# Soft-routing mixture of experts on one core: five instead of four pairs of P1 in front, four instead of six mixed stages, six instead of five pairs of P2, and B21's casts spread over 56 slots instead of 44

## The chip, the core and the metric

The kernel runs on one core of a Trainium2 chip. The metric is the device time of one execution in microseconds (us). The core's engines are named as in its profile: PE (TensorE, the matrix unit; PEld is its weight load), DVE (VectorE), ACT (ScalarE), POOL (GpSimd, which here only issues DMAs, those with a change of type among them) and SP (SyncE, which issues DMAs). Each engine takes its instructions strictly in order. SBUF is the on-chip memory that all engines read, PSUM the accumulator memory that PE writes (eight banks of 128 x 512 float32 here).

## The reference

```
batch, seq, hidden, n_experts, expert_hidden = 16, 512, 512, 8, 2048
probs = softmax(router_logits)                  # over the 8 experts
for e in range(n_experts):
    expert_out = np.matmul(x, expert_weights[e])
    output += probs[:, :, e:e+1] * expert_out
```

All 8 experts see every token. Scaling a token's row of x by its probability and putting the eight scaled copies side by side makes it one product: a left matrix of 8192 rows (tokens) by 4096 (8 experts x 512 hidden) with the stacked weights, 4096 by 2048. Inputs and output are float32; the products run in float16 with float32 sums.

## The kernel before

**Two levels of Strassen's method (Winograd's form).** At the upper level the rows are split into 16 blocks q of 512 tokens, each with an even and an odd half of 256 tokens; the contraction is split into the experts 0 to 3 and 4 to 7; the output columns into two halves of 1024. A weight quadrant is B11, B12, B21 or B22 (first digit the half of the experts, second digit the half of the columns). Seven products P1 to P7 for each q take the place of eight. P1 is x's even half, scaled by the probabilities of the experts 0 to 3, times B11; P2 is the same rows, scaled for the experts 4 to 7, times B21. The first output block of a q is P1 + P2. P1 alone is needed again later, in the base of P6, and so goes to a DRAM buffer `kept` as well.

**One product** (`Product`) is again seven inner steps, in the order of `STEPS` (1, 5, 6, 2, 7, 3, 4). A step is eight 128x128 by 128x512 matmuls into one PSUM bank. Its left operand is a tile `z` (or `d`, a difference) that DVE makes from x and the probabilities (`Left`, `times`), its right operand a weight tile `w`. Each product gives four output tiles `h` of 128 x 512 float32, called (0, 0), (0, 1), (1, 0), (1, 1). A product without a base (P1) leaves PSUM by ACT copies and two DVE additions (`post_alone`). A product with a base (P2) takes the base tile, already in SBUF, and DVE adds PSUM to it in place at six of the seven steps (`post_on_base`). A finished tile is stored by `pool(...)`, a DMA on POOL's queue.

**Stages.** `add(product, product)` makes a stage of two products, whose steps take turns: 14 slots of one step. In the trace a stage of two products takes 24.17 us, a slot 1.73 us. P1 of q = 0 and 1 is computed in a plain way in the beginning, before stage 0. Stages 0 to 3 are pairs of P1 (q = 2 to 9), stages 4 to 9 are mixed (P2 of q beside P1 of q + 1, for q = 9 to 14), stages 10 to 14 are pairs of P2 alone (15 and 0, 1 and 2, and so on to 7 and 8). After them come the pairs of P5 and P6, of P6 and P7, P4 and P7, and P3.

In a mixed stage the base of P2 of q is the tile `h` in which P1 of the same q was left one stage before, `products[1, q].o`, which stays in SBUF. In a pair of P2 the base has to be read back from `kept` by a DMA on SP's queue (`Base.fetch`, `fetch_at`), except for q = 15. x blocks work alike: a mixed stage reuses the transposed block `xT` of P1, a pair of P2 alone loads it again from DRAM (`x_dram`).

**Hooks and weights.** `at(stage, slot, make)` hangs work at a slot. The four blocks of B21 are cast from float32 to float16 by DMAs on POOL's queue (`cast21`, two DMAs of 512 KB each), `sums_at` puts the three sums of them (2.28 us of DVE each, in place of four tiles seven) in the last stage of P1 pairs. From the first mixed stage on, six "wedges" (`wedge_at`) follow at one for each stage: at slot 2 two casts of 512 KB, at slot 11 three DVE operations (1.21 us each) whose results go to DRAM in three stores of 512 KB (`wd`); B12 and B22 give the later right operands t1, t2, t3 this way. The part ODD of these is cast apart: B12 at stage 9 slot 9, B11 at stage 10 slot 2, B22 at stage 10 slot 9 (`cast_odd`, two DMAs of 512 KB each), combined by three DVE operations of 2.28 us from stage 11 slot 6 on (`odd_t`). Stage 11 also fetches three t1 blocks of 1 MB on ACT's queue (`fetch_at_w`).

**Buffers and queues that set the order.** `hpool` has 12 buffers for `h`; `wpool` has 15 for `w`. A fetch of a base takes the next buffer of `hpool`, and SP waits until the store that read the buffer last has landed. POOL's DMAs use eight semaphores in turn, so that each waits until the one eight before it has landed: at most eight are under way. DVE's work is put in order by a small planner (`later`, `slack`, `need`) that knows a cost for each task and a clock for PE.

Of the kernel before, what the change touches and what calls it, by code (L numbers as in the profile page):

```python
# [31 lines left out]
def kernel(  # L32
# [87 lines left out]
    def pool(o, i, **how):  # L120
        note(nc.gpsimd.dma_start(out=o, in_=i, **how))  # L121
# [26 lines left out]
    def cast_block(q, kn, t=None, parts=1):  # L148
        t = new_w() if t is None else t
        for e in range(2):  # L150
            cast_w(q, kn, e, t[:, ds(e * C, C), :], parts if e == 0 else 1)
        return t
# [204 lines left out]
    def need(task):  # L357
        if task is not None and not task.done:
            flush(task)
            clock["pe"] = max(clock["pe"], clock["dve"])  # L360

    def later(cost, make, first=False):
        t = Task(cost, make)
        (queue.appendleft if first else queue.append)(t)
        return t
# [181 lines left out]
                tt(o[tn], q if p in (5, 3) else x, base, ADD)  # L547


    def out_rows(q, odd, cols, tn):  # L550
        t, n = tn
        return out_f[ds((2 * q + odd) * HQ + t * HP, HP), ds(cols * NH + n * NB, NB)]

    def to_out(q, odd, cols, **how):
        return lambda tn, o: pool(out_rows(q, odd, cols, tn), o, **how)
# [20 lines left out]
    def at(stage, slot, make):  # L576
        hooks.setdefault((stage, slot), []).append(make)

    def add(*products):
        stages.append(products)  # L580
        return len(stages) - 1
# [11 lines left out]
    def left_of(r, q, fresh=True):  # L593
        a, b = 2 * q, 2 * q + 1
        if r == 1:
            pt = PBlock(a, P1, xp1[q - 2][1] if q in (2, 3) else None)
            if q in (2, 3):
                xs[a] = XBlock(a, xp1[q - 2][0])
            return Left(xblock(a), pt), [xblock(a), pt]
        if r in (2, 4):  # L600
            h, pt = (a, PBlock(a, P2)) if r == 2 else (b, PBlock(b, P2))
            return Left(xblock(h), pt), [xblock(h), pt]
        if r == 5:
            pt = PBlock(b, PQ)
            return Left(xblock(b), pt), [xblock(b), pt]
        if r == 6:
            pt = PBlock(a, P1)
            return Left(xblock(a), pt, of=lefts[5, q]), [xblock(a), pt]
        pa, pb = PBlock(a, P1 if r == 7 else PQ), PBlock(b, P1 if r == 7 else PQ)
        return Left(xblock(a), pa, (xblock(b), pb)), [xblock(a), pa, xblock(b), pb]  # L610

    def kept_rows(q):
        return lambda tn: kept[q][tn[1], ds(tn[0] * HP, HP), :]

    def product(r, q, **how):
        left, loads = left_of(r, q)
        lefts[r, q] = left
        p = None
        if r == 1:
            def sink(tn, o):  # L620
                pool(kept_rows(q)(tn), o)
            p = Product(right[1], left, sink)
        elif r == 2:
            if q >= 9:
                base = products[1, q].o.__getitem__
            else:
                base = bases[2, q] = Base(kept_rows(q))
            p = Product(right[2], left, to_out(q, 0, 0), base)
        elif r == 5:
            bases[6, q] = m1 = Base(kept_rows(q))  # L630
            m1.task = {}

            p = Product(right[5], left, to_out(q, 1, 0))
        elif r == 6:
            m1 = bases[6, q]

            def base(tn):
                need(m1.task[tn])
                return m1.t[tn]
            p = Product(right[6], left, to_out(q, 0, 1), base)  # L640
        elif r == 7:
            base = bases[7, q] = Base(lambda tn: out_rows(q, 0, 1, tn))
            p = Product(right[7], left, to_out(q, 1, 1), base)
        elif r == 4:
            p = Product(right[4], left, to_out(q, 1, 0, accum_op=ADD), products[7, q].o.__getitem__)
        else:
            p = Product(right[3], left, to_out(q, 0, 1, accum_op=ADD), **how)
        p.loads = loads
        products[r, q] = p
        return p  # L650

    products = {}
    forget = lambda *hs: [xs.pop(h, None) for h in hs]
# [53 lines left out]
    def fetch_at(stage, slot, base, *tns):  # L707
        for tn in tns:
            at(stage, slot, lambda tn=tn: base.fetch(tn))


    for q in (2, 4, 6, 8):
        add(product(1, q), product(1, q + 1))
    for q in range(9, 15):
        add(product(2, q), product(1, q + 1))
    forget(*range(0, 18, 2))
    rest = [15] + list(range(9))
    for i in range(0, 10, 2):
        k = add(product(2, rest[i]), product(2, rest[i + 1]))
        for slot, tn in zip((8, 10, 12, 13), INNER):  # L720
            for q in rest[i:i + 2]:
                if q < 9:
                    fetch_at(k if tn == (1, 0) else k - 1, 3 if tn == (1, 0) else slot, bases[2, q], tn)
    xs.clear()
    k5 = add(product(5, 0), product(5, 1))
# [37 lines left out]
    def wedge(kn, e):  # L763

        t = new_w()
        a, b = t[:, ds(0, C), :], t[:, ds(C, C), :]
        rows = ds(e * C, C)

        def casts():
            cast_w(12, kn, e, a)  # L770
            cast_w(22, kn, e, b)

        def send(what, u):
            pool(kept_w(what, kn)[:, rows, :], u)

        def t3():
            u = new_u().rearrange("p (c two) t -> p c (two t)", two=2)
            tt(u, b, a, SUB)
            send("t3", u)

        def t1():
            tt(a, b11[kn][:, rows, :], a, SUB)
            send("t1", a)

        def t2():
            tt(b, b, a, ADD)
            send("t2", b)
        return casts, [t3, t1, t2]

    def wedge_at(stage, slot, kn, e, then):  # L790
        made = []

        def begin():
            casts, made_ = wedge(kn, e)
            casts()
            made.extend(made_)

        def go_on():
            for make in made:
                later(1.22, make)  # L800
        at(stage, slot, begin)
        at(*then, go_on)

    b21, t1, t2, t3 = {}, {}, {}, {}

    def cast21(kn):
        b21[kn] = cast_block(21, kn)

    for i, kn in enumerate(((0, 0), (0, 1), (1, 1), (1, 0))):
        at((11 * i + 8) // 14, (11 * i + 8) % 14, lambda kn=kn: cast21(kn))  # L810

    def sums_at(stage, slot, r, of, ps):
        def go():
            if right[r].w is None:
                right[r].sums = right[r].build(of)
            for p in ps:
                right[r].queue_sum(right[r].sums, p)
        at(stage, slot, go)
    sums_at(3, 3, 2, b21, (5,))
    sums_at(3, 5, 2, b21, (6,))  # L820
    sums_at(3, 7, 2, b21, (7,))
    sums_at(3, 12, 2, b21, (4,))
    for i, (kn, e) in enumerate((kn, e) for kn in ((0, 0), (1, 0), (1, 1)) for e in range(2)):
        wedge_at(4 + i, 2, kn, e, (4 + i, 11))

    def fetch_at_w(stage, slot, of, what, kn):
        at(stage, slot, lambda: of.__setitem__(kn, fetch_w(what, kn)))
# [141 lines left out]

    finish = products[3, 15]  # L970
    finish.base = Base(lambda tn: out_rows(15, 0, 1, tn))
    finish.sink = lambda tn, o: sp(out_rows(15, 0, 1, tn), o)
    for slot, tn in zip((6, 8, 10, 12), INNER):
# [73 lines left out]
```

## Time and profile before

| what | value |
|---|---|
| median of 3 runs | 1375.59 us (1375.47 to 1375.77) |
| the profiled execution | 1376.63 us, its span (first to last instruction) 1374.9 us |
| mean granted TensorE clock | 1.000 |
| PE busy | 1367.3 us, 99% of the span |
| DVE busy | 1108.6 us, 81% |
| POOL busy (issuing DMAs) | 411.8 us, 30% |
| ACT busy | 183.1 us, 13% |
| moved by DMA | 338.02 MB, mean 246 GB/s |

Busy times are sums over one engine; an engine can be busy while nobody waits for it. A wait is told as "who waited <- what ended the wait". The stages below are told by their place in the span: stage 0 begins at 41.0 us, and each stage of two products is 24.17 us long, so that stage 9 is 258.60 to 282.77, stage 10 is 282.77 to 306.94, stage 11 is 306.94 to 331.12 and stage 12 is 331.12 to 355.29. A DMA has a time of issue and a time of landing; the time between the two is told with it.

### The profile page before, as it was taken

Reading aid. Unit: us, or ns where it says so; the run is one execution under the profiler, and the core shown is the slowest. Engines: PE = TensorE matmul, PEld = TensorE weight load, DVE = VectorE, ACT = ScalarE, POOL = GpSimd, SP = SyncE. Lnnn points to the kernel's source line nnn. Section 1 sums busy time; section 2 is a strip of 40 time slices with the busy share of each in tenths; the row PEclk is TensorE's granted clock in tenths of the full one; section 3 lists DMA queues with packets and bytes.
Section 4 is the critical chain, followed back from the end, with each engine's and each line's share of the span. In section 5 each row is a group of like instructions: output and inputs, shape, how many; then the busy total and the mean of one; then the engine's idle time right before and its main releaser. Section 6 shows DMA issues by size and latency. Waiting matters only on the chain.

```text
span 1374.9 us, 17480 instructions
## 1 busy us (share of the span) xinstructions
PE 1367.3 (99%) x6390; PEld 622.0 (45%) x6390; DVE 1108.6 (81%) x1290; ACT 183.1 (13%) x317; POOL 411.8 (30%) x652
## 2 busy tenths in 40 slices
PE   8999999999999999999999999999999999999998
PEld 4444444444444444444444444444444444444444
DVE  5846757669889888798897988889889898988882
ACT  3222111100011111111111100000000000222221
POOL 3222333241223342334232122242333322232221
PEclk9999999999999999999999999999999999999999
DMA  9998999999898998899898998988898979987786
GB/s 183 222 261 205 211 248 265 241 299 378 240 323 249 285 300 246 259 261 265 245 276 263 338 392 219 224 236 212 229 237 223 247 204 316 249 187 177 166 150 106
DMA packets 191271, 338.02 MB, mean 246 GB/s; under 512 B 52944, under 2 KB 86992, under 8 KB 187472
## 3 DMA queue, kind: packets, MB, share of 16 engines
q0 software_dynamic: 88688, 185.12, 55.8%
q1 hardware_dynamic: 98464, 123.34, 30.8%
q10 hardware_dynamic: 4032, 28.44, 5.3%
q8 instruction: 50, 0.82, 0.2%
q14 instruction: 37, 0.30, 0.1%
HBM read 207.65 MB, written 156.43 MB: 265 GB/s over the span
## 4 chain that ended last, share of the span: by engine, by line
PE 98%; DMA 2%; POOL 0%; issue 0%; ACT 0%; POOLq 0%
PE ps L127 98%; DMA w<-wd 1%; DMA w<-in_expert_weights_dram 1%; POOL w L121 0%; ACT h L999 0%; POOL ident L211 0%; POOLq L211 0%; POOLq L1031 0%
## 5 line engine op out<-in xcount | busy, mean ns | idle before, releaser
L127 PE MATMUL ps<-w,z 128*128 128x512 f16 x5416 | 1177.3, 379 | 1.3 <-DMA w<-in_expert_weights_dram 1.1
L127 PEld LDWEIGHTS <-z 128*128 128x128 f16 x5416 | 529.7, 98 | 638.6 <-DMA w<-in_expert_weights_dram 1.3
L121 POOL DMA_DIRECT2D out_dram<-h x380 | 248.9, 672 | 746.4 <-ACT h L540 373.7
L107 DVE TENSOR_TENSOR h<-ps,h 128x512 f32<-128x512 f32 x415 | 282.5, 687 | 207.6 <-PE ps L127 192.8
L107 DVE TENSOR_TENSOR z<-xT,pT 128x2048 f16<-128x2048 f16 x220 | 266.8, 1216 | 11.5 <-DMA xT<-xs 6.3
L127 PE MATMUL ps<-w,d 128*128 128x512 f16 x880 | 199.1, 379 | 0.0
L127 PEld LDWEIGHTS <-d 128*128 128x128 f16 x880 | 86.1, 98 | 103.8
L107 DVE TENSOR_TENSOR z<-z,d 128x2048 f16<-128x2048 f16 x110 | 132.1, 1215 | 0.0
L107 DVE TENSOR_TENSOR w<-w 128x1024 f16<-128x1024 f16 (+2 forms) x92 | 100.8, 1102 | 5.1 <-DMA wd<-w 3.4
L527 ACT COPY h<-ps 128x512 f32<-128x512 f32 x90 | 52.8, 586 | 373.4 <-PE ps L127 336.3
L540 ACT COPY h<-ps 128x512 f32<-128x512 f32 x64 | 37.5, 587 | 486.3 <-PE ps L127 459.9
L107 DVE TENSOR_TENSOR d<-z 128x1024 f16<-128x1024 f16 x110 | 75.2, 685 | 6.8 <-PE ps L127 5.0
L107 DVE TENSOR_TENSOR z<-z,u 128x2048 f16<-128x2048 f16 x64 | 78.4, 1225 | 2.2
L107 DVE TENSOR_TENSOR u<-xT,pT 128x2048 f16<-128x2048 f16 x64 | 77.9, 1217 | 0.0
L523 ACT COPY h<-ps 128x512 f32<-128x512 f32 x90 | 52.8, 587 | 173.9 <-PE ps L127 162.5
L121 POOL DMA_DIRECT2D w<-in_expert_weights_dram x65 | 49.0, 785 | 33.8 <-DMA wd<-w 24.0
L121 POOL DMA_DIRECT2D wd<-w x86 | 48.3, 585 | 36.0 <-DVE w L107 26.4
L107 DVE TENSOR_TENSOR ps<-ps,h 128x512 f32<-128x512 f32 (+1 forms) x66 | 45.3, 688 | 13.0 <-PE ps L127 13.0
L121 POOL DMA_DIRECT2D kept<-h x56 | 30.8, 551 | 76.8 <-ACT h L527 48.2
L107 DVE TENSOR_TENSOR h<-h 128x512 f32<-128x512 f32 (+2 forms) x69 | 45.1, 674 | 0.1
L519 ACT COPY ps<-ps 128x512 f32<-128x512 f32 x45 | 25.6, 570 | 114.6 <-PE ps L127 114.6
L107 DVE TENSOR_TENSOR z<-z 128x2048 f16<-128x2048 f16 x32 | 39.2, 1225 | 1.1
(47 smaller groups left out, 97.0 us busy)
## 6 DMA issues: line engine op xcount, KB each, us to landing
out_dram<-h POOLq DMA_DIRECT2D x380, 256.0 KB, 6.2
pT<-p_dram SPq DMA_DIRECT2D x140, 256.0 KB, 6.0
w<-wd ACTq DMA_DIRECT2D x27, 1024.0 KB, 9.9
h<-kept SPq DMA_DIRECT2D x100, 256.0 KB, 5.6
xT<-x SPq DMA_DIRECT2D x87, 256.0 KB, 5.5
wd<-w POOLq DMA_DIRECT2D x72, 256.0 KB, 5.5
w<-in_expert_weights_dram POOLq DMA_DIRECT2D x35, 512.0 KB, 10.1
h<-out_dram SPq DMA_DIRECT2D x68, 256.0 KB, 5.6
```

The lines of the kernel that those rows point to most:

```text
L107: dve(nc.vector.tensor_tensor(out=o, in0=a, in1=b, op=op))
L121: note(nc.gpsimd.dma_start(out=o, in_=i, **how))
L127: note(nc.tensor.matmul(ps, z, w, start=start, stop=stop, skip_group_check=True))
L519: act(nc.scalar.copy(self.banks["b"], x))
L523: act(nc.scalar.copy(o[tn], q if p == 5 else x))
L527: act(nc.scalar.copy(o[TN[p]], b if p == 2 else x))
L540: act(nc.scalar.copy(o[tn], b))
```

## The change

The border `QK` between the q whose P1 is done in front and those done beside P2 goes from 9 to 11. Stages 0 to 4 are now pairs of P1 (q = 2 to 11), stages 5 to 8 are mixed (q = 11 to 14), and stages 9 to 14 are pairs of P2 alone (15 and 0, then 1 and 2, to 9 and 10). The number of stages stays the same, and nothing behind stage 14 is edited. P2 of q = 9 and 10 now has its base fetched from `kept`. What hung at the last P1 stage (the sums of B21) and at the mixed stages (the six wedges) goes one stage later with the border, to `ND - 1` = 4 and `ND + i` = 5 to 10. The casts of ODD, `odd_t` and the fetches of t1 stay at the stages they had. B21's four casts hang at slots 8, 22, 36 and 50, counted through, in place of 8, 19, 30 and 41.

```diff
+    QK = 11
+    ND = QK // 2
+
...
-            if q >= 9:
+            if q >= QK:
                 base = products[1, q].o.__getitem__
             else:
                 base = bases[2, q] = Base(kept_rows(q))
...
-    for q in (2, 4, 6, 8):
+    for q in range(2, QK, 2):
         add(product(1, q), product(1, q + 1))
-    for q in range(9, 15):
+    for q in range(QK, 15):
         add(product(2, q), product(1, q + 1))
-    forget(*range(0, 18, 2))
-    rest = [15] + list(range(9))
-    for i in range(0, 10, 2):
+    forget(*range(0, 2 * QK, 2))
+    rest = [15] + list(range(QK))
+    for i in range(0, QK + 1, 2):
         k = add(product(2, rest[i]), product(2, rest[i + 1]))
         for slot, tn in zip((8, 10, 12, 13), INNER):
             for q in rest[i:i + 2]:
-                if q < 9:
+                if q < QK:
                     fetch_at(k if tn == (1, 0) else k - 1, 3 if tn == (1, 0) else slot, bases[2, q], tn)
...
     for i, kn in enumerate(((0, 0), (0, 1), (1, 1), (1, 0))):
-        at((11 * i + 8) // 14, (11 * i + 8) % 14, lambda kn=kn: cast21(kn))
+        at((14 * i + 8) // 14, (14 * i + 8) % 14, lambda kn=kn: cast21(kn))
...
-    sums_at(3, 3, 2, b21, (5,))
-    sums_at(3, 5, 2, b21, (6,))
-    sums_at(3, 7, 2, b21, (7,))
-    sums_at(3, 12, 2, b21, (4,))
+    sums_at(ND - 1, 3, 2, b21, (5,))
+    sums_at(ND - 1, 5, 2, b21, (6,))
+    sums_at(ND - 1, 7, 2, b21, (7,))
+    sums_at(ND - 1, 12, 2, b21, (4,))
     for i, (kn, e) in enumerate((kn, e) for kn in ((0, 0), (1, 0), (1, 1)) for e in range(2)):
-        wedge_at(4 + i, 2, kn, e, (4 + i, 11))
+        wedge_at(ND + i, 2, kn, e, (ND + i, 11))
```

## The prediction

> **What bounds the kernel now.** I read the page's busy times first, then its groups of PE, then the chain that ended last, and last the stretches of 24.17 us (one stage of two products) around the edit.
>
> ```profile
> PE 1367.3 (99%) x6390; PEld 622.0 (45%) x6390; DVE 1108.6 (81%) x1290; ACT 183.1 (13%) x317; POOL 411.8 (30%) x652
> ...
> L127 PE MATMUL ps<-w,z 128*128 128x512 f16 x5416 | 1177.3, 379 | 1.3 <-DMA w<-in_expert_weights_dram 1.1
> ```
> ```profile
> 10.75 775.35 PE ps L127 x3616
> 786.10 14.93 DMA w<-wd
> 801.02 0.05 issue
> 801.07 570.07 PE ps L127 x2648
> ```
>
> A busy PE is not yet a PE at its pace, so I also took the distance between matmul starts from the trace: 216 ns for nearly all of the 128x512 ones. After the prologue only one distance is longer, 518 ns at 800.55 us: a weight fetch (the DMA in the chain above) landed 0.3 us late. So from 41.0 us on (stage 0), PE runs 110 products of 56 x 0.2158 = 12.09 us with 0.3 us lost. PE's instructions are the same in the changed kernel, in number and order, and so is every engine's order up to stage 1. **No gain above 0.3 us is to be had; the only question is whether the change makes PE wait.** How near it is to waiting shows in these stretches (columns: PE, PEld, DVE, ACT, POOL busy, clock, DMA share, GB/s), for stages 9 to 12:
>
> ```profile
> 258.60:282.77 24.17, 24.17 (x114) 10.93 (x112) 16.72 (x20) 3.50 (x6) 9.53 (x17) 1.00 1.08 270
> 282.77:306.94 24.17, 24.17 (x113) 10.98 (x112) 15.61 (x20) 1.76 (x3) 8.02 (x14) 1.00 1.13 293
> 306.94:331.12 24.18, 24.18 (x114) 10.94 (x113) 22.22 (x23) 1.18 (x2) 5.20 (x10) 1.00 1.04 347
> 331.12:355.29 24.17, 24.17 (x114) 10.97 (x112) 20.15 (x22) 1.17 (x2) 4.33 (x8) 1.00 0.90 347
> ```
>
> PE is full in each, DVE has 2 us to spare in the worst, and the DMA engines are full from stage 9 to 11 (shares of the queues add up to over 1). The DMA view of stage 10 alone, in 40 slices of 0.6 us, and what SP waited for in stages 10 and 11:
>
> ```profile
> GB/s 290 283 288 256 214 283 290 215 225 259 400 400 427 420 420 420 414 420 414 359 203 244 300 307 242 214 207 246 290 273 207 217 258 341 378 225 175 236 231 220
> ...
> out_dram<-h POOLq DMA_DIRECT2D x8, 256.0 KB, 12.5
> w<-in_expert_weights_dram POOLq DMA_DIRECT2D x4, 512.0 KB, 11.0
> h<-kept SPq DMA_DIRECT2D x4, 256.0 KB, 6.3
> ```
> ```profile
> SPq L118 <- DMA out_dram<-h: 40.8, 11, 10.0
> ```
>
> A store takes 12.5 us from issue to landing here; in stage 4 the same view gives 4.1. Every fetch of a base waits for a store to free one of the 12 `h` buffers: 40.8 us in 11 waits. That is the resource which the change touches.
>
> **Parts that cost nothing, and what covers them.** DVE, ACT and POOL keep their instruction counts. SP gets ten more DMAs of 256 KB: eight bases (`h<-kept`, q = 9 and 10) and two `xT<-x`. The second P1-pair stage more needs two x blocks where a mixed stage needs one; those transposed blocks are made two stages ahead, and DVE was busy for 12.56 us in stage 1 and 11.38 us in stage 2, so that it can wait for one some 10 us before PE's next step is short. B21's four sums (4 x 2.28 us) move with the last P1 stage, whose DVE time was 17.55 of 24.17 us; spreading the casts over more slots thins stages 1 and 2, where PE waits for nothing. All zero; without this cover, each late x block would cost what it is late beyond 10 us.
>
> At the old hand-over from mixed to P2 alone, DVE waited for P1's store of q = 15, issued on POOL's queue behind the B12 casts of ODD:
>
> ```profile
> 291.00 0.69 DVE L107 TENSOR_TENSOR h<-ps,h 128x512 f32<-128x512 f32 x1 [2.68 <-DMA kept<-h]
> ```
>
> The hand-over goes to stage 9, one stage ahead of these casts. PE had a margin left there (1.96 us at its smallest), so that this gain is zero too.
>
> **The part that costs: the last wedge meets the casts of ODD.** ODD's casts stay (two DMAs in stage 9 and four in stage 10, two of these at slot 2), but the last wedge moves from stage 9 to 10: two casts more at that same slot 2, ahead of ODD's on POOL's queue, and three stores of 512 KB at its end. Stage 9 becomes a pair of P2 that fetches ten bases. The prices, from the slices above: copies alone run at 420 GB/s, so 256 KB cost 0.62 us of all DMA engines, 512 KB 1.25, 1 MB 2.5; in the slices with casts 512 KB land at 214 GB/s, 2.45 us; `xs` (256 KB cast) half of it. For each stage I add up what the program issues in it:
>
> Before. Stage 9: 20 transfers of 256 KB (12.4), 3 stores of 512 KB (3.7), 4 casts (9.8), one xs (1.2): 27.1 us. Stage 10: 24 (14.9), one store (1.2), 4 casts (9.8): 25.9. Stage 11: 19 (11.8) and four of 1 MB (9.9): 21.7. Stage 12: 8.7. Against 24.17 us a stage, what is left over at the ends: 3.0, 4.7, 2.3, 0.
>
> After. Stage 8: 22.2 (before: 16.7). Stage 9: 23 (14.3), 3 stores (3.7), 4 casts (9.8): 27.8. Stage 10: 20 (12.4), 3 stores (3.7), 6 casts (14.7): 30.8. Stage 11: 19, one more store of 512 KB, four of 1 MB: 22.9. Stage 12: 9.3. Left over: 0, 3.6, 10.3, 9.0, 0.
>
> So stores and the buffers they free come 10.3 - 4.7 = 5.6 us later around the end of stage 10 and 9.0 - 2.3 = 6.7 us later around the end of stage 11. Against this stands the slack. The tightest bases landed 3.8 us before DVE's addition in stage 11 (both (0, 1) tiles), 4.6 and 1.9 us in stage 12. PE takes up the same bank some time after the addition:
>
> ```profile
> 341.69 0.68 DVE L107 TENSOR_TENSOR h<-ps,h 128x512 f32<-128x512 f32 x1
> ```
>
> This one (the one with 1.9 us) ends at 342.37, and PE comes back to its bank at 346.65: 4.3 us. Stage 11: 3.8 + 4.3 = 8.1 us against 5.6, no stall. Stage 12: 1.9 + 4.3 = 6.2 against 6.7, a stall of **0.5 us**. A stall of PE is paid once, since everything behind it gets the same time, and stage 12 has 15 us of DMA time to spare.
>
> Bounds of the cast's price, as the trace shows no cast beside so many others: a copy of the bytes landed (1.25) leaves nothing over in either kernel, 0 us; the mean distance between landings of casts that followed each other in stage 10 with other DMAs between (up to 3.65) gives 9.6 us later instead of 6.7, a stall of 3.4. I take 2.45, from the slices of this very stage. The sum against the profiled execution's own time: 1376.63 + 0.5 = 1377.1; it stands 1.04 us above the median of the runs, so 1375.59 + 0.5 = 1376.1 us.
>
> [...]
>
> **Rivals.** *(1) The backlog is paid twice.* The store that frees a buffer is late and then the fetch into it is late as well. For it: fetches of stage 12's bases took 10.3 us, against 5.6 over the whole kernel. Against it: in stage 10 fetches took 6.3 us while POOL's stores took 12.5. If the fetch adds half of the delay again, 6.7 x 1.5 = 10.0, less 6.2, is 3.8 us: 1379.4; with all of it, 7.2 us. It decides from the point where stage 12's (0, 1) bases land over 6.2 us later than before. [...]
>
> *(2) DVE waits for the last wedge's cast.* DVE reached a wedge's first operation at 254.22 in stage 8; two stages later that is 302.57. The casts at that place of POOL's queue (ODD's B11) landed at 301.60 and 304.14, so DVE will wait about 1.6 us in front of the additions that PE needs next. With PE's 4.3 us that costs nothing up to 306.9; if the 5.6 us of backlog come ahead of the cast, it lands at 309.7 and PE loses 2.8 us: 1378.4. Against it: POOL's content up to these casts is 0.5 MB less than before.
>
> *(3) Faster.* The 0.3 us at 800 us would have to go, by luck in the later timing: 1375.3, still no change by the bound below. Faster by more would need the prologue, which is not edited.
>
> **How the numbers follow.** About 0.2% (2.75 us) is what a measurement of this kernel can tell from no change. The forecast, a stall from none to 2.7 us, (3) among it: 57%. Rival (1): 27%. Rival (2): 14%. Something that the profile does not show makes it faster: 2%. So faster 0.02, same 0.57, slower 0.41. The time is that of the forecast, 1376.1. The range reaches from 1375.2 (nothing lost, and the 0.3 us gained) to 1381.0, over (1) at 1379.4 and (2) at 1378.4 and part of the way to (1)'s 7.2 us.
>
> **What would show it right or wrong.** Right: PE busy for all of each stretch up to stage 9; DMA share and store times higher in stage 10 (about 18 us to landing, from 12.5); DVE waiting for `w<-in_expert_weights_dram` in stage 10 and for `h<-kept` in stages 11 and 12, where it had not; any stall of PE in stages 10 to 12 and nowhere else. Wrong: a stall in stages 0 to 8 (x blocks or sums), or no longer store times in stage 10, or waits of SP for stores that grow by far more than 7 us.

## The result and the profile after

| | before | after |
|---|---|---|
| median | 1375.7 us (1375.47 to 1376.85, 6 runs) | 1384.11 us (1382.88 to 1386.82, 6 runs) |
| profiled execution, its span | 1376.63, 1374.9 us | 1383.64, 1381.9 us |

The ratio is 1.0063 [1.005, 1.0076]: the change makes the kernel slower by 8.4 us. The forecast of 1376.1 us is wrong, and the range up to 1381.0 us does not hold the time.

The busy times and the groups of the page after, to be laid beside those of before:

```profile
PE 1370.7 (99%) x6390; PEld 622.9 (45%) x6390; DVE 1108.5 (80%) x1290; ACT 182.8 (13%) x317; POOL 411.5 (30%) x652
...
L127 PE MATMUL ps<-w,z 128*128 128x512 f16 x5416 | 1179.4, 379 | 5.7 <-DVE h L107 5.2
```

The work is the same on every engine. PE's idle time before its matmuls has grown from 1.3 to 5.7 us and has another releaser: DVE's additions to `h`. The same matmuls are also busy for 2.1 us longer. Where to look is in the chain that ended last (start, length, what; only some of its longest pieces are printed):

```profile
18.34 259.20 PE ps L127 x1212
...
282.06 15.08 DMA out_dram<-h
...
337.38 12.48 DMA out_dram<-h
349.90 0.70 DVE h L107
350.64 1027.59 PE ps L127 x4760
```

From 277 to 350 us the chain leaves PE, mainly for four stores on POOL's queue, of 12.5 to 15.1 us each by the chain; before and behind that it is PE alone. It says where to look and no more: its last store was issued at 337.38 us and landed at 350.73, when the addition that it is said to release (349.90) had long begun. The weight fetch at 786 us, which cost 0.3 us before, is no longer in it. The stretches of stages 9 to 12 (columns as in the prediction: PE, PEld, DVE, ACT, POOL busy, clock, DMA share, GB/s):

```profile
258.60:282.77 24.17, 24.17 (x114) 10.97 (x113) 18.52 (x23) 1.73 (x3) 9.05 (x15) 1.00 0.99 286
282.77:306.94 24.17, 24.17 (x114) 10.93 (x113) 14.83 (x20) 1.17 (x2) 7.28 (x11) 1.00 1.12 303
306.94:331.12 24.18, 22.36 (x103) 9.93 (x102) 21.16 (x24) 1.17 (x2) 6.50 (x12) 1.00 1.11 331
331.12:355.29 24.17, 20.70 (x89) 8.93 (x88) 17.83 (x21) 1.17 (x2) 3.79 (x8) 0.93 1.02 391
```

PE is full up to 306.94 us and loses time in the last two rows only. By the distances between matmul starts, the gaps are 0.26 us at 313.41, 1.43 at 320.58, 0.62 at 328.91 and 3.63 at 346.80: 5.9 us. The clock column of the last row, 0.93, is the rest. The same view in shorter pieces, one around the gap, one from 1.2 us behind it, one behind that:

```profile
346.60:350.64 4.04, 0.58 (x3) 0.18 (x2) 1.99 (x5) 0.58 (x1) 0.89 (x2) 1.00 1.03 394
351.83:355.24 3.41, 3.41 (x10) 1.18 (x8) 3.38 (x5) 0.00 (x0) 0.00 (x0) 0.50 0.98 290
355.24:359.00 3.76, 3.76 (x18) 1.66 (x17) 3.76 (x5) 0.00 (x0) 0.54 (x1) 1.00 0.98 354
```

For 3.41 us the granted clock is 0.50, with matmuls 427 ns apart in place of 216; that costs 1.7 us. Gaps and clock make 7.6 us, less the 0.3 us gained at 800 us: 7.3 of the span's 7.0. What DVE waited for from 258.6 to 360 us (total, times, longest):

```profile
DVE h L107 <- DMA h<-kept: 7.2, 2, 4.3
DVE u L107 <- DMA w<-in_expert_weights_dram: 4.4, 1, 4.4
DVE h L107 <- DMA out_dram<-h: 2.1, 1, 2.1
```

None of these three waits was there before. The third is put down to a store that landed at 349.77, after the addition had begun (348.70); the base of that addition landed at 348.57, so this is a wait for `h<-kept` too. The old wait for `kept<-h` at the hand-over (2.68 us) is gone, and no wait for it came at the new hand-over. In the time line of DVE they stand as idle time in brackets in front of the operation (start, length):

```profile
306.80 1.23 DVE L107 TENSOR_TENSOR u<-w 128x2048 f16<-128x2048 f16 x1 [4.37 <-DMA w<-in_expert_weights_dram]
...
321.48 0.69 DVE L107 TENSOR_TENSOR h<-ps,h 128x512 f32<-128x512 f32 x1 [2.99 <-DMA h<-kept]
...
344.82 0.69 DVE L107 TENSOR_TENSOR h<-ps,h 128x512 f32<-128x512 f32 x1 [4.25 <-DMA h<-kept]
...
348.70 0.69 DVE L107 TENSOR_TENSOR h<-ps,h 128x512 f32<-128x512 f32 x1 [2.05 <-DMA out_dram<-h]
...
349.90 0.69 DVE L107 TENSOR_TENSOR h<-ps,h 128x512 f32<-128x512 f32 x1
```

The first is the last wedge's first operation, which was ready at 302.4 us. Its two casts were issued at 292.23 and 292.98 us and landed at 303.40 and 306.68. DVE's next operations start late by that much, and PE's gap of 0.26 us at 313.41 is what it costs; the rest is covered by the margin that PE has on DVE.

The second is a base of stage 11, the first product's (0, 1), and PE's gap of 1.43 us ends with it. Its fetch was issued at 314.02 us and landed at 321.35. It had waited for the store that frees its buffer, which was issued at 296.45, before DVE's wait began, and landed at 313.97. In the kernel before that store took from 295.94 to 306.19 us and the fetch from 306.24 to 311.97. So the wait for the cast has no part in this gap. The gap of 0.62 us follows from it: DVE has no idle time from 321.48 us to the addition that PE then waits for.

Nor did the wait for the cast delay a store that stage 12's bases waited for. From POOL's time line:

```profile
303.68 0.76 POOL L121 DMA_DIRECT2D w<-in_expert_weights_dram  x1 [2.75 <-DMA w<-in_expert_weights_dram]
307.26 0.56 POOL L121 DMA_DIRECT2D out_dram<-h  x1 [2.83 <-DMA w<-in_expert_weights_dram]
309.80 0.56 POOL L121 DMA_DIRECT2D out_dram<-h  x1 [1.98 <-DVE w L107]
```

The third row stores a tile whose addition ended at 302.43 us. It was issued 0.59 us after the landing, at 309.22, of the DMA eight before it on POOL's queue. Below, a DMA of POOL counts as held when it was issued less than 0.8 us after the landing of the one eight before. In the changed kernel 21 of POOL's 23 DMAs in stages 10 and 11 were held, all of them from 287.47 to 324.32 us; in the kernel before 6 of 22. What DVE had ready there waited for POOL, not the other way round.

From the DMA view of stage 10, to be held against that of before:

```profile
w<-in_expert_weights_dram POOLq DMA_DIRECT2D x6, 512.0 KB, 16.1
...
out_dram<-h POOLq DMA_DIRECT2D x4, 256.0 KB, 16.1
```

A store takes 16.1 us (12.5 before), a cast 16.1 (11.0). And from 327 to 340 us, when stage 12's last bases are fetched, with the three 1 MB blocks of t1 on ACT's queue:

```profile
w<-wd ACTq DMA_DIRECT2D x3, 1024.0 KB, 9.4
h<-kept SPq DMA_DIRECT2D x4, 256.0 KB, 15.1
```

Before, the same span has one 1 MB fetch and three bases at 9.7 us. The gap of 3.63 us ends with the addition at 349.90 us, that of the first product's (0, 1). Its base was issued at 325.10 us and landed at 335.34 before; now it is issued at 334.58 and lands at 349.70. That is 14.4 us later: 9.5 because the store that frees its buffer landed late, 4.9 because its own transfer takes 15.1 in place of 10.3. The addition ahead of it on DVE (348.70) is late as well: its base, the second product's (1, 1), landed at 348.57 us in place of 324.22, 24.4 later. The last base, the second product's (0, 1), came 11.1 us later (350.92 in place of 339.82), and DVE, by then behind, did not have to wait for it.

So there are two places, and in both PE waits mainly for base tiles. In stage 11 it loses 2.3 us, 0.26 of them by the wait for the last wedge's cast. In stage 12 the bases are later still, and PE loses 3.6 us and 1.7 us of clock.

### The profile page after: what moved, and what is told of

Its sections match the earlier page's. It is cut to its first block, busy times and chain, and to the rows that moved or that the text cites. A ratio compares the mean times of both kernels' runs of the same rounds, so it can differ in the third digit from the quotient of the medians.

```text
span 1381.9 us, 17505 instructions
## 1 busy us (share of the span) xinstructions
PE 1370.7 (99%) x6390; PEld 622.9 (45%) x6390; DVE 1108.5 (80%) x1290; ACT 182.8 (13%) x317; POOL 411.5 (30%) x652
## 4 chain that ended last, share of the span: by engine, by line
PE 93%; DMA 5%; issue 1%; POOL 1%; DVE 0%; ACT 0%; POOLq 0%; DVEq 0%
PE ps L127 93%; DMA out_dram<-h 3%; DMA wd<-u 1%; DMA w<-in_expert_weights_dram 1%; POOL w L121 0%; POOL out_dram L121 0%; DVE h L107 0%; POOL wd L121 0%; DVE u L107 0%; ACT h L1002 0%; POOL ident L211 0%; POOLq L121 0%; POOLq L211 0%; DVEq L107 0%; POOLq L1034 0%
```

## The experiments

Theory A of the first expectations is the prediction's own mechanism, the last wedge beside ODD's casts, with a larger size: the last wedge's casts and stores make a backlog that is paid in stages 11 and 12. In what follows, "no gap" means that no distance between matmul starts behind stage 0 stands more than 0.3 us above 0.216 us.

**All wedges one stage earlier, in the changed kernel.**

```diff
-        wedge_at(ND + i, 2, kn, e, (ND + i, 11))
+        wedge_at(ND - 1 + i, 2, kn, e, (ND - 1 + i, 11))
```

> The changed kernel, but with the six wedges at stages 4 to 9 as before the change, so that the last one no longer shares stage 10 with ODD's casts. Theory A (the stalls come from the last wedge's two casts and three stores on top of ODD's casts, a backlog of DMA): back to within 1 us of the kernel before, 1375.5 to 1376.7, no gap in PE over 0.3 us in stages 9 to 13. Theory B (the stalls come from the border itself: two more pairs that fetch their bases, ten more DMAs on SP's queue, 12 h buffers): 1380 or more, with PE's gaps in stages 11 and 12 still there.

Measured: 1375.85 us, ratio to before 0.9998 [0.9988, 1.0007]; no gap. PE is full in stages 11 and 12:

```profile
306.94:331.12 24.18, 24.18 (x113) 10.94 (x112) 22.20 (x24) 1.17 (x2) 5.93 (x11) 1.00 1.07 348
331.12:355.29 24.17, 24.17 (x113) 10.97 (x112) 20.00 (x23) 1.17 (x2) 4.32 (x8) 1.00 0.96 360
```

The whole loss hangs on the wedges' place, as theory A has it; 10 of POOL's 22 DMAs in stages 10 and 11 are held. x blocks, B21's sums, the fetched bases and the hand-over, all still as in the changed kernel, cost nothing. Stage 12's fetches still take up to 16.3 us here; but the last two are issued at 325.25 and 328.59 us and land at 341.50 and 343.07, early enough.

**ODD's casts one stage earlier, in the changed kernel.**

```diff
-    for stage, slot, q in ((9, 9, 12), (10, 2, 11), (10, 9, 22), (last2, 8, 21)):
+    for stage, slot, q in ((8, 9, 12), (9, 2, 11), (9, 9, 22), (last2, 8, 21)):
```

> The changed kernel, but with ODD's three casts one stage earlier too (stage 8 slot 9, stage 9 slots 2 and 9), so that they stand to the wedges as before the change. Theory A: no PE gap over 0.3 us in stages 10 to 13, 1375.5 to 1377. Theory B: the backlog is that of the fetching pairs, which now meet the casts a stage earlier: 1380 or more.

Measured: 1384.56 us, 1.0058 [1.0043, 1.0073]: no better. Theory A missed, and the number that theory B gives came by a mechanism that neither names. What DVE waited for:

```profile
DVE u L107 <- DMA w<-in_expert_weights_dram: 13.2, 2, 11.1
```

POOL's order now has all of ODD's casts ahead of the last wedge's. With eight DMAs under way at most, the wedge's cast was issued only at 297.82 us and landed at 313.40. DVE waited 11.1 us for it, and PE had gaps of 3.54 us (311.60) and 3.48 us (316.87), the second followed by half clock; stage 12 is full. This is the prediction's second rival, in pure form. It also gives its price: the wait less the gaps, 11.13 - 3.54 - 3.48, is a margin of 4.11 us, and the changed kernel's 4.37 - 0.26 gives the same 4.11.

**The last wedge in stage 10 in the kernel before.**

```diff
-        wedge_at(4 + i, 2, kn, e, (4 + i, 11))
+        wedge_at(4 + i + i // 5, 2, kn, e, (4 + i + i // 5, 11))
```

> The kernel before with one part of the change alone: the last wedge at stage 10 in place of 9. Border, fetches and B21's casts stay. Theory A: most of the loss is there, 1380 to 1385, with PE gaps in stages 11 and 12. Theory B: within 1 us of the kernel before.

Measured: 1375.75 us, 0.9995 [0.9986, 1.0004]; no gap. Theory A missed here. Stages 9 and 10 of this run:

```profile
258.60:282.77 24.17, 24.17 (x114) 10.97 (x113) 14.65 (x18) 3.49 (x7) 7.15 (x12) 1.00 0.83 237
282.77:306.94 24.17, 24.17 (x114) 10.93 (x113) 17.32 (x22) 1.27 (x3) 9.00 (x15) 1.00 1.17 259
```

With no wedge in stage 9 (DMA share 0.83) POOL is not behind when stage 10 begins: the casts were issued at 283.69 and 286.05 us and landed at 295.05 and 299.06, before DVE asked. The last wedge beside ODD's casts is therefore not enough. By the prediction's sum this kernel ends stages 10 and 11 with 10.3 and 7.9 us left over, about the changed kernel's 10.3 and 9.0; so that sum does not separate a kernel that loses nothing from one that loses 8 us. The count of held DMAs does separate the two: 10 of POOL's 26 here, 21 of 23 there.

**B21's casts at their old spacing, in the changed kernel.**

```diff
-        at((14 * i + 8) // 14, (14 * i + 8) % 14, lambda kn=kn: cast21(kn))
+        at((11 * i + 8) // 14, (11 * i + 8) % 14, lambda kn=kn: cast21(kn))
```

> The changed kernel with B21's casts at slots 8, 19, 30 and 41 again. Theories A and B: as the changed kernel, 1383 to 1387. A theory C, that the spread of B21's casts takes part: over 1 us away from it.

Measured: 1383.89 us, 1.0053 [1.0036, 1.0069]: the interval overlaps that of the change. The gaps are the same two places' (0.13 and 0.62 us in stage 11, 6.33 us at 345.19, with half clock from within the gap on). 18 of POOL's 23 DMAs in stages 10 and 11 are held. The spacing is no part of the loss.

**The last wedge's casts in stage 9 (slot 4), in the changed kernel.**

```diff
-        wedge_at(ND + i, 2, kn, e, (ND + i, 11))
+        wedge_at(ND + i - i // 5, 2 + i // 5 * 2, kn, e, (ND + i, 11))
```

> The changed kernel, but the last wedge's two casts are issued at stage 9 slot 4 in place of stage 10 slot 2; its DVE work and its three stores stay at the end of stage 10. The DMA work of stages 9 to 11 is the same in sum, and nothing is left out. Theory D (sum: the backlog at the end of stage 10 and in stage 11 decides, wherever in stages 9 and 10 the casts stand): DVE no longer waits for the cast, but the bases of stages 11 and 12 are still late, PE idle of 3 us or more there, 1380 to 1385. Theory E (place: what decides is that DVE waits for this cast in stage 10, and that it stands ahead of stage 10's stores): no PE gap over 0.5 us, 1375.5 to 1377.

Measured: 1378.98 us, 1.0018 [1.0008, 1.0028]. Both expectations missed. The wait for the cast is gone, and stage 11 is full; in stage 12 one gap of 2.50 us (344.66) is left, again with half clock behind it in the profiled execution, which at 1381.24 us was the longest of the ten and has a gap of 0.91 us at 804.68 besides. The place of the casts accounts for some 6 of the 8.4 us, more than stage 11's 2.3: earlier casts bring stage 12's bases forward too (12 of POOL's 26 DMAs are held, and the (0, 1) bases land at 346.51 and 347.13 us). What stays is in stage 12.

**ODD's B11 casts behind the stores, in the changed kernel.**

```diff
-    for stage, slot, q in ((9, 9, 12), (10, 2, 11), (10, 9, 22), (last2, 8, 21)):
+    for stage, slot, q in ((9, 9, 12), (10, 12, 11), (10, 9, 22), (last2, 8, 21)):
```

> The changed kernel, but ODD's casts of B11 are issued at stage 10 slot 12 in place of slot 2, so that they stand behind six of stage 10's eight stores on POOL's queue and no longer right behind the last wedge's casts. The sum of DMA work is the same. Theory D (sum): the stores that free stage 11's buffers land some 5 us sooner, but those that free stage 12's as late as in the changed kernel; PE loses 3 us or more in stage 12, 1380 or more. Theory E (place): the loss in stage 11 goes, the wait for the wedge's cast stays (4 us of DVE), PE loses under 2 us: 1376 to 1378.

Measured: 1386.39 us, 1.0074 [1.0059, 1.0089]. Both expectations missed. DVE still waited 5.11 us for the wedge's cast (it landed at 307.36 us), with a gap of 1.00 us at 313.34, the margin of 4.11 once more. The moved cast landed at 332.10 us and held `odd_t`, and with it the additions behind it on DVE: a gap of 6.74 us at 328.17. Only 10 of POOL's 21 DMAs are held here: this loss is another one. In both orders that were run, somebody misses the casts that are put back.

**ODD's B12 casts in stage 8, in the changed kernel.** The third experiment says that stage 9 must be full too. This one relieves stage 9 and leaves the last wedge where it is.

```diff
-    for stage, slot, q in ((9, 9, 12), (10, 2, 11), (10, 9, 22), (last2, 8, 21)):
+    for stage, slot, q in ((8, 9, 12), (10, 2, 11), (10, 9, 22), (last2, 8, 21)):
```

> After, with ODD's B12 casts (two of 512 KB, 4.9 us of all DMA engines by the prediction's price) at stage 8 slot 9 in place of stage 9 slot 9. The last wedge stays in stage 10. Theory F (the last wedge's casts land late because stage 9, now a pair with fetched bases, is also full, and that POOL's eight in flight hold them back): they land by 302.6 us, DVE does not wait for them, PE has no gap in stage 11; what is left is at most a gap of 2.5 us with a stretch of half clock in stage 12: 1376 to 1380 us. Theory G (the last wedge beside ODD's casts in stage 10 is enough by itself): DVE waits some 4 us for the cast as before, PE loses about 2 us in stage 11 and 5 in stage 12: 1383 to 1385 us.

Measured: 1382.36 us, 1.0045 [1.0028, 1.0062]. The casts were issued at 286.09 and 286.84 us, six us earlier, and landed at 300.63 and 303.56; DVE waited 1.8 us in place of 4.4. The bases that PE had waited for in stage 11 landed at 316.79 and 318.79 us in place of 321.35 and 323.07, and stage 11 is full, as theory F had it:

```profile
306.94:331.12 24.18, 24.18 (x114) 10.94 (x112) 22.42 (x24) 1.17 (x2) 6.80 (x13) 1.00 1.09 350
331.12:355.29 24.17, 19.79 (x92) 8.78 (x90) 15.68 (x18) 1.17 (x2) 2.71 (x5) 1.00 0.98 381
```

Its time was missed: stage 12 has gaps of 3.76, 0.95 and 0.62 us all the same. The first place goes with stage 9's load (13 of POOL's 27 DMAs in stages 10 and 11 are held); the second does not.

**The fetches of t1 later, in the changed kernel.** Moved are the three 1 MB fetches and the sums that read them (in the changed kernel these sums ran from 355.23 us on, behind the gap in stage 12).

```diff
-        fetch_at_w(11 + (8 + 4 * i) // 14, (8 + 4 * i) % 14, t1, "t1", kn)
+        fetch_at_w(12 + (6 + 4 * i) // 14, (6 + 4 * i) % 14, t1, "t1", kn)
...
-    sums_at(12, 8, 5, t1, (5, 6))
-    sums_at(13, 2, 5, t1, (7, 4))
+    sums_at(13, 4, 5, t1, (5, 6))
+    sums_at(13, 10, 5, t1, (7, 4))
```

> After, with the three 1 MB fetches of t1 on ACT's queue 12 slots later (stage 12 slots 6 and 10, stage 13 slot 0, in place of stage 11 slots 8 and 12 and stage 12 slot 2), and the sums that read them 10 slots and 8 slots later. Theory H (the fetches of stage 12's bases take 14 to 16 us because 1 MB transfers run beside them, and this is the second payment): these fetches take under 10 us, the gap of 3.6 us in stage 12 and the half clock behind it go, the gaps in stage 11 (2.3 us in all) stay: 1377.5 to 1379.5 us. Theory I (the bases are late because the stores that free their buffers are late; the 1 MB fetches add little): a gap in stage 12 stays at over 2 us with its half clock: 1382 to 1384 us.

Measured: 1377.85 us, 1.001 [1.0001, 1.002]. The first of the three was issued at 327.02 us all the same (ACT had nothing ahead of it), the other two at 347.43 and 349.92. From 327 to 340 us:

```profile
w<-wd ACTq DMA_DIRECT2D x1, 1024.0 KB, 8.1
h<-kept SPq DMA_DIRECT2D x4, 256.0 KB, 10.8
```

Stage 12's last base was issued at 335.78 us, 1.3 us earlier than in the changed kernel, and landed at 345.37, 5.6 us earlier. The gap of 3.63 us shrinks to 0.31 us and the half clock goes; gaps in stage 11 stay (0.29, 0.57 and 0.62 us), 18 of POOL's 23 DMAs are still held, and DVE's wait for the cast, 4.01 us here, left no gap. The time lies in theory H's range, though three of the four fetches still took over 10 us. The clearest case is the base that ended the gap: it was issued at 334.54 us, as in the changed kernel (334.58), and took 10.2 us in place of 15.1. The transfers beside the bases, not the late issue alone, make stage 12's loss.

**Both: the last wedge's casts in stage 9 and the t1 fetches later.** The edits of the last experiment and of the one with the casts at slot 4 together.

> After, with both: the last wedge's casts and stores in stage 9, and the t1 fetches and their sums later. If the two places (the cast that DVE waits for, and stage 12's fetches) are all of the loss: no gap of PE above 0.3 us in stages 10 to 12, 1375.3 to 1377 us, with a ratio to before that holds 1. If something else is left of the 2.3 us that the earlier cast alone left over, a gap in stages 10 to 12 stays: 1378 us or more.

Measured: 1375.98 us, 0.9996 [0.9987, 1.0005]; no gap. What DVE waited for, other than PE, from 258.6 to 360 us:

```profile
DVE h L107 <- DMA h<-kept: 1.8, 2, 1.4
DVE h L107 <- DMA wd<-w: 0.7, 1, 0.7
```

The two places are all of the loss; 10 of POOL's 24 DMAs are held. (Made singly, the two edits left 2.4 and 1.5 us of the loss, each against the runs of the kernel before taken with it. So they took off some 6.1 and 6.9 us of the 8.4, more than all of it, as each relieves stage 12.) Nothing is gained over the kernel before, from which this version can't be told apart; no version that was run beats it.

**DVE blocked, in the kernel before**, to price a gap of PE by itself. At stage 13 slot 5 DVE gets n more products that write a spare tile (n = 6, then 8).

```diff
+    def delay():
+        u, left = new_u(), lefts[2, 5]
+        for _ in range(6):
+            times(u, 0, left.xb, left.pb)
+    at(13, 5, delay)
```

> The kernel before with six more DVE products (1.21 us each, into the tile u, results unused) at stage 13 slot 5, to hold up PE once. DVE is blocked for 7.3 us, PE's margin is 4.3 us and DVE is idle for about 1 us before the next addition that PE needs: PE idles for about 2 us. If an idle stretch costs its own length only, the time is 1.8 to 2.5 us above the kernel before, at full clock throughout; if the clock falls after any stall, 1.7 us more.

> The same with eight products: DVE is blocked for 9.7 us, PE idles for about 4.4 us. If the clock falls after an idle stretch of this length, as it did behind the 3.6 us in the changed kernel, the time is 6 us above the kernel before, with 3.4 us at half clock; if an idle stretch costs its length only, 4.4 us above.

Measured, in one run each: 1380.59 us with a gap of 3.21 us, 1385.51 us with one of 5.74 us (and one of 0.44 at 809 us). The pieces at half clock, of n = 6 and then of n = 8:

```profile
373.05:376.46 3.41, 2.67 (x7) 0.99 (x7) 3.41 (x5) 0.00 (x0) 0.00 (x0) 0.50 0.99 335
```
```profile
375.42:382.25 6.83, 5.98 (x15) 2.12 (x15) 6.83 (x7) 0.00 (x0) 0.54 (x1) 0.50 0.41 137
```

The gaps were expected at about 2 and 4.4 us, and the surcharge of 1.7 us behind the first was left open. With 1376.63 us for the kernel before beside them, 3.21 us of gap cost 1380.59 - 1376.63 = 4.0 us, and 5.74 us (6.2 with the later one) cost 8.9. These gaps of PE cost more than their length.

## Why the prediction was wrong

**What held.** No gain was to be had: no version is faster than before, and the 0.3 us at 800 us did go, by luck. The parts said to cost nothing cost nothing (with all of them in place, the first experiment and the one with both edits lose nothing). PE stalls in stages 11 and 12 only, and the waits of DVE that were named came where they were named: for the cast in stage 10, for `h<-kept` in stages 11 and 12. The stores of stage 10 were said to take about 18 us; they took 16.1.

**The step that failed: "So stores and the buffers they free come 10.3 - 4.7 = 5.6 us later around the end of stage 10 and 9.0 - 2.3 = 6.7 us later around the end of stage 11", and with it "Stage 11: 3.8 + 4.3 = 8.1 us against 5.6, no stall" and "Stage 12: 1.9 + 4.3 = 6.2 against 6.7, a stall of 0.5 us."** The slack was about right; the delays were not.

In stage 11 the first product's (0, 1) base came 9.4 us later, not 5.6. That is 1.3 over the 8.1 us of slack, and PE's gap was 1.43. In stage 12 the bases of (1, 1) and (0, 1) came 21.8, 24.4, 14.4 and 11.1 us later, not 6.7. The prediction looked at the last of these, which had the least slack; by its arithmetic 11.1 against 6.2 is a stall of 4.9. The one that PE waited for was the first product's (0, 1): it had 4.6 + 4.3 = 8.9 us of slack and came 14.4 later, 5.5 over. The gaps of stages 11 and 12 together were 5.9.

The 5.6 and 6.7 came from a sum of DMA time over a whole stage, in which each byte delays each other byte equally. The runs show that it is not so: with about the same sum, the kernel before with its last wedge in stage 10 lost nothing (1375.75 us), and moving two 1 MB fetches away, behind the tightest bases, took off most of the loss (1377.85 us). Two things that the sum does not have decide. One is POOL's limit of eight DMAs under way: in stages 10 and 11 it held 21 of 23 in the changed kernel, and 10 of 22 to 26 in the three versions that lose nothing. The other is what runs beside a transfer in the 10 to 16 us before somebody needs it: issued at the same time, the base that ended stage 12's gap took 15.1 us beside the 1 MB fetches and 10.2 with two of the three moved behind it. A sum of waits hides it too: SP's waits for stores in stages 10 and 11, which the prediction names as a sign, grew only from 40.8 to 44.8 us.

**The first rival was the answer.** The condition that it set for "the backlog is paid twice", (0, 1) bases over 6.2 us later, was met with 14.4 and 11.1. The fetch added about half of the store's delay again (4.9 to 9.5), as in the lower of its two prices; only the delay that it started from, 6.7, was too small. The evidence set against it, that fetches took 6.3 us in stage 10 while stores took 12.5, came from a stage in which no 1 MB transfer ran beside them. The three that do run beside stage 12's fetches stood in the sum as 7.5 us of bytes and nowhere as neighbours.

**The second rival came too, and cost little.** DVE waited 4.4 us for the last wedge's cast, not 1.6, and PE lost 0.26 us by it, not 2.8: the cast came at 306.68 us, and "that costs nothing up to 306.9" was right. Both rivals have one cause, the backlog on POOL's queue from the end of stage 9 on, but each was given a chance of its own, as if only one could come.

**"A stall of PE is paid once"** is wrong as well. Behind the gap of 3.63 us the clock was 0.50 for 3.41 us, 1.7 us more; the last experiments show a surcharge without the rest of the change (4.0 us for a gap of 3.21, 8.9 for 6.2 us of gaps). Gaps and clock, less the 0.3 us gained, make 7.3 us; the two profiled executions differ by 7.0, the medians by 8.4. Of the changed kernel's six executions the three longest have a mean granted clock of 0.997 or 0.998, the three shortest, the profiled one among them, 0.999.

**What stays open.** The third experiment shows that the last wedge beside ODD's casts is not enough for the first place, and the seventh that relieving stage 9 is enough there. The limit of eight was not varied, so how much of the lateness comes from it and how much from the other transfers on the DMA engines (shares of 1.12, 1.11 and 1.02 in stages 10 to 12) is not known. How much of stage 12's lateness comes from the last wedge's three stores and how much from its two casts was not tried, nor whether more buffers for `h` would absorb it.

## What to carry to other kernels

When a change makes a busy stretch of DMAs longer, look for every place where somebody waits for one of them: waits with one cause can come together and need not be alternatives (here DVE waited 4.4 us for a cast, and 7.2 and 2.1 us for bases). A sum of bytes over a stage says that there is a backlog; who pays is read from the single transfer, from what is ahead of it on its queue, how many that queue may have under way (eight here), and which large transfers run beside it (15.1 us for one base here, 10.2 with two such moved away). Do not follow only the transfer with the least slack: one with more can come later still (here 14.4 us late against 11.1). And a gap of PE can cost more than its length: behind the 3.63 us here half of a 3.41 us stretch came on top, 1.7 us. Its length alone did not decide whether it did, as the next section shows.

## What the hardware showed that was not expected

In these profiles the half clock came in stretches of 3.41 us: one with gaps of 2.50, 3.21, 3.48 and 3.63 us, two on end (6.83 us) with 5.74, 6.33 and 6.74 us (with 3.21 us and the last three it set in within the gap itself). In the changed kernel it began at 351.83 us, 1.19 us after PE had come back (350.64). Behind 3.54 us (the first gap with all of ODD's casts earlier) and 3.76 us (B12 in stage 8) none came. So the length of the gap alone does not decide, and what decides besides it was not shown.

The granted clock differs between executions of one kernel too: in the experiment with the casts in stage 9, the four longest of the ten (1379.22 to 1381.24 us) have a mean clock of 0.999, the other six (1377.31 to 1379.10) of 1.000.
